# Another distance, within 512 bytes, between the rows of the split operands and the rows of the weights

## The chip, the cores and the metric

One core of a Trainium2 chip. The metric is the device time in microseconds of one execution on that core. The kernel before has a median of 1011.47 us over 3 runs (1011.46, 1011.47 and 1014.0).

## What is computed

Two transformer blocks one after the other, on 256 tokens of width 1024, in float32. The first has two kinds of attention, a merge and a feed-forward part; the second a chunked delta rule, a sparse attention, an output projection `w_out`, a cross-attention to 256 memory tokens and a feed-forward part. What matters here are the dense products in them:

```python
# first block
merged = g_swa * (o_swa @ w_branch_swa[l]) + g_diff * (o_diff @ w_branch_diff[l])
h = h + rms_norm(merged @ w_out[l], post_mix_gain[l])
u = rms_norm(h, pre_ffn_gain[l])
gate_up = u @ w_ffn_in[l]
f = (jax.nn.silu(gate_up[..., :D_FF]) * gate_up[..., D_FF:]) @ w_ffn_out[l]
# second block
x = x + jnp.concatenate([o_dn, o_dsa], axis=-1) @ w_out[l]
hx = rmsnorm(x, g_xattn[l]);  mn = rmsnorm(mem, g_mem[l])
qx = hx @ w_xq[l];  kvx = mn @ w_xkv[l]
x = x + ox @ w_xo[l]
hf = rmsnorm(x, g_ffn[l])
x = x + (jax.nn.silu(hf @ w_gate[l]) * (hf @ w_up[l])) @ w_down[l]
```

## The kernel before

Activations lie transposed, as 8 row tiles of 128 features by 256 tokens (`KT` = 8, `NT` = 256; `NK` = 272 where the 16 meta tokens of the first block stand behind them). A product of an activation with 128 columns of a weight matrix is one call of `gemm` (L316). `load_w` (L301) has SP fetch the 512 KB of those columns into `raw`, ACT round them to float32r (`wh`) and DVE, or POOL in the first stages, subtract to get the rest (`wl`); there are three buffers of each, or more where the planner of the tiles finds room. The activation was split in the same way before, by `split` (L284), into a high part and a low part. `gemm` then issues 24 matmuls into one PSUM tile: for each of the 8 row tiles `wh` against the high part and `wh` against the low part, then for each row tile `wl` against the high part. In each of these matmuls TensorE loads a square of 128x128 weights (stationary) and streams the 256 columns of one row tile of the activation past it (moving). The next square is loaded while a matmul streams.

The split operands, and who uses them:

- `uh`, `ul` from `new_u` (L406): 8 row tiles of `NK` = 272 floats each, so that row tile k begins 1088 k bytes into the tile, and 256 of the 272 are used after the first stage. Made in `post_norm` (L851) for the 44 gemms of the first feed-forward part (`ffn_in`, L871, called at L914), and in `residual` (L1522) for the 8 gemms of `w_xq` (L1565) and for the 44 gemms of the second feed-forward part (L1621). A first pair (L421) feeds the projections of the first block.
- `mem_h`, `mem_l` (L771): 8 row tiles of 256 floats, 1024 bytes each. They are the moving operand in the 8 gemms of `mem_keys` (L787) and the stationary one in `mem_values` (L791, 8 weight tiles with 24 matmuls each at L802 to L804; three of the four groups run at L930, the last is woven into the second block).
- `mix_h`, `mix_l` (L957) for the 8 gemms of `w_out` of the second block (L1536); `ox_h`, `ox_l` (L1553) for the 8 gemms of `w_xo` (L1602).
- `f_h`, `f_l`: moving in `post_norm` for `w_fo1` (L925), stationary in `down` (L1628) for `w_dn`.
- `od_h`/`m_h` and their low parts, and `os_h`, `os_l`, as the moving operand of other gemms.

Where a tile begins is chosen by the planner when the program is built. In the program of the kernel before, counted modulo 512 bytes within a partition, all `raw`, `wh` and `wl` begin at 192, and as a square of weights has rows of 512 bytes, so does every square. Against that the row tiles of the split operands lie, in bytes:

| operand | distance from the weights' rows, modulo 512 |
|---|---|
| `f_h`, `f_l`, `m_h`, `m_l`, `od_h`, `od_l` | -64, the same for every row tile |
| `mem_h`, `mem_l`, `ox_h`, `ox_l` | 0, the same for every row tile |
| `mix_h` / `mix_l` | -64 / 0 |
| `uh`, `ul` of both feed-forward parts | 0, 64, 128, ... 448: 64 more with each row tile (the row tiles are 1088 bytes apart) |
| `uh`, `ul` of `w_xq` | -64, 0, 64, ...: 64 more with each row tile |

Of the kernel before, what the change touches and what calls it, by code (L numbers as in the profile page):

```python
# [17 lines left out]
F32R = mybir.dt.float32r  # L18
# [7 lines left out]
P = 128  # L26
NT = 256
NM = 16
NK = NT + NM
NP = NT + 32  # L30
D = 1024
KT = D // P
FF = 2816
FT = FF // P
# [177 lines left out]
BDLAST = 0  # L212
WARM = 12
RB = 2
MAGIC = float(0x5F3759DF)
# [5 lines left out]
def _program(tc, d, out):  # L221
# [10 lines left out]
    with ctx:  # L232
# [4 lines left out]
        gpool = new_pool(ctx, "gen")  # L237
# [3 lines left out]
        hT = rpool.tile([P, KT, NK], F32, name="hT", tag="resA")  # L241
# [164 lines left out]
        def new_u():  # L406
            uh = gpool.tile([P, KT, NK], F32R, name="uh", tag="uh")
            ul = gpool.tile([P, KT, NK], F32R, name="ul", tag="ul")
            return uh, ul


# [9 lines left out]
        uh, ul = new_u()  # L421
# [6 lines left out]
        for k in range(1, KT, 2):  # L428
            n = min(2, KT - k)
# [16 lines left out]
        rs = gpool.tile([P, NK], F32, name="rs", tag="rs", bufs=2)  # L446
        rsqrt_chain(st[:, :NK], NK, rs)
        us = [(uh[:, k, :NT], ul[:, k, :NT]) for k in range(KT)]
# [34 lines left out]
        at = ExitStack()  # L483
# [286 lines left out]
        mhp = new_pool(mhst, "memhl", side="right")  # L770
        mem_h = mhp.tile([P, 8, NT], F32R, name="mem_h")  # L771
        mem_l = mhp.tile([P, 8, NT], F32R, name="mem_l")
        memt = mhp.tile([P, KT, NT], F32, name="memt")
# [36 lines left out]
        mpool = new_pool(mg, "m")  # L810
# [25 lines left out]

        def post_norm(src_w, xs, gain, res, res_out, g_next, whole=False):

# [9 lines left out]
            if whole:  # L848
                u = gpool.tile([P, KT, NK], F32, name="u", tag="uh")
            else:  # L850
                uh, ul = new_u()  # L851
            acc2 = gpool.tile([P, NK], F32, name="acc2", tag="acc2", bufs=1)[:, :NT]
# [10 lines left out]
            if whole:  # L863
                return [u[:, k, :NT] for k in range(8)], rs2[:, :NT]
            return [(uh[:, k, :NT], ul[:, k, :NT]) for k in range(8)], rs2[:, :NT]

        h1 = rpool.tile([P, KT, NT], F32, name="h1", tag="resB")
        us, rs = post_norm(d["w_out1"], [(m_h[:, k, :], m_l[:, k, :]) for k in range(8)],
                           "post_mix", hT, h1, "pre_ffn")

# [23 lines left out]
        bpool = new_pool(b2, "b")  # L894
# [16 lines left out]
        mpool = new_pool(fst, "f")  # L911
        f_h = mpool.tile([P, FT, NT], F32R, name="f_h")
# [43 lines left out]
        dve.memset(ones_q, 1.0 / 256)  # L956
        mix_h = bpool.tile([P, 8, NT], F32R, name="mix_h")  # L957
        mix_l = bpool.tile([P, 8, NT], F32R, name="mix_l")

# [560 lines left out]

        def residual(src_w, xs, res, res_out, g_next, late=(), more=0):
            uh, ul = new_u()  # L1522
            acc = gpool.tile([P, NK], F32, name="acc", tag="acc", bufs=1)[:, :NT]
# [10 lines left out]

        x2 = rpool.tile([P, KT, NT], F32, name="x2", tag="resB")
        us, rs = residual(d["w_out2"], [(mix_h[:, k, :], mix_l[:, k, :]) for k in range(8)], x1, x2, "g_xattn", (0,1,2,3), 2)  # L1536
        b2.close()

# [13 lines left out]
        values = [two("vx_", vx[:, :, h * NT:(h + 1) * NT]) for h in range(4)]  # L1552
        ox_h = xpool.tile([P, 8, NT], F32R, name="ox_h")  # L1553
        ox_l = xpool.tile([P, 8, NT], F32R, name="ox_l")
        rx = xpool.tile([P, 4], F32, name="rx")
# [45 lines left out]
        x3 = rpool.tile([P, KT, NK], F32, name="x3", tag="resA")[:, :, :NT]  # L1601
        us, rs = residual(d["w_xo"], [(ox_h[:, k, :], ox_l[:, k, :]) for k in range(8)], x2, x3, "g_ffn", (4,5,6,7), 2)  # L1602
        xa.close()
# [9 lines left out]
        for qb in range(2):  # L1613
            for kk_ in range(2):
# [3 lines left out]
                dve.tensor_copy(x3t[:, qb, kk_ * 512:(kk_ + 1) * 512], t)  # L1618
        f_h = mpool.tile([P, FT, NT], F32R, name="f_h")
        f_l = mpool.tile([P, FT, NT], F32R, name="f_l")  # L1620
        ffn_in(mpool, d["w_gu2"], us, rs, f_h, f_l)  # L1621
# [77 lines left out]
```

## Time and profile before

| | |
|---|---|
| median of 3 runs | 1011.47 us (1011.46 to 1014.0) |
| the profiled execution's own time | 1014.09 us |
| its span, first to last instruction | 1012.3 us |
| TensorE matmul busy | 974.1 us, 96% of the span |
| weight loads on TensorE busy | 916.1 us, 90% |
| VectorE, ScalarE, GpSimd busy | 722.8, 544.8, 312.3 us |
| mean granted TensorE clock | 0.984 |

The span lies 1.8 us under the profiled execution's own time. A matmul's record lasts longer than the time to the next one's start, as they are pipelined: a 128x256 record lasts some 280 ns and the next one starts after some 115 ns. What counts for the time is the distance from start to start, which the text calls the pitch.

### The profile page before, as it was taken

Reading aid. Unit: us, or ns where it says so; the run is one execution under the profiler, and the core shown is the slowest. Engines: PE = TensorE matmul, PEld = TensorE weight load, DVE = VectorE, ACT = ScalarE, POOL = GpSimd, SP = SyncE. Lnnn points to the kernel's source line nnn. Section 1 sums busy time; section 2 is a strip of 40 time slices with the busy share of each in tenths; the row PEclk is TensorE's granted clock in tenths of the full one; section 3 lists DMA queues with packets and bytes.
Section 4 is the critical chain, followed back from the end, with each engine's and each line's share of the span. In section 5 each row is a group of like instructions: output and inputs, shape, how many; then the busy total and the mean of one; then the engine's idle time right before and its main releaser. Section 6 shows DMA issues by size and latency. Waiting matters only on the chain. (4 is left out here: it accounts for less than half of the span.)

```text
span 1012.3 us, 18979 instructions
## 1 busy us (share of the span) xinstructions
PE 974.1 (96%) x7356; PEld 916.1 (90%) x7356; DVE 722.8 (71%) x1468; ACT 544.8 (54%) x1089; POOL 312.3 (31%) x294
## 2 busy tenths in 40 slices
PE   9889999999978999999999899999999999999996
PEld 8779999998978999999999788787799999999885
DVE  7998899887697696656455638977687676666444
ACT  4556677666544555555454444335666555555433
POOL 6865468655491032221100302221021002222002
PEclk9998999999997999999999899999999999999998
DMA  6333333333434555555666232333045255555552
GB/s 238 129 104 101 109 107 124 120 110 105 167 125 148 188 204 186 187 187 183 214 200 198 83 133 91 122 114 106 1 150 205 64 186 188 187 187 186 182 192 88
DMA packets 42026, 149.31 MB, mean 147 GB/s; under 512 B 4728, under 2 KB 5376, under 8 KB 41808
## 3 DMA queue, kind: packets, MB, share of 16 engines
q1 hardware_dynamic: 40896, 145.47, 42.6%
q0 software_dynamic: 608, 2.03, 0.7%
q8 instruction: 58, 0.95, 0.4%
q10 hardware_dynamic: 432, 0.59, 0.2%
q14 instruction: 32, 0.26, 0.1%
HBM read 147.01 MB, written 1.06 MB: 146 GB/s over the span
## 5 line engine op out<-in xcount | busy, mean ns | idle before, releaser
L311 ACT ACTIVATE wh<-raw 128x1024 fp32r<-128x1024 f32 (+1 forms) x244 | 256.2, 1052 | 222.7 <-PE mm L326 134.3
L313 DVE TENSOR_TENSOR wl<-raw,wh 128x1024 fp32r<-128x1024 f32 (+1 forms) x220 | 274.0, 1247 | 85.8 <-ACT wh L311 83.7
L326 PE MATMUL mm<-uh,wh 128*128 128x256 f32 (+1 forms) x1112 | 280.5, 287 | 1.3 <-DVE vbm L540 0.9
L326 PE MATMUL mm<-ul,wh 128*128 128x256 f32 (+1 forms) x1112 | 279.0, 286 | 0.2 <-DVE ul L291 0.2
L326 PEld LDWEIGHTS mm<-uh,wh 128*128 128x128 f32 x1112 | 211.1, 190 | 4.6 <-DVE vbm L540 1.1
L326 PEld LDWEIGHTS mm<-ul,wh 128*128 128x128 f32 x1112 | 211.5, 190 | 1.3 <-DVE ul L291 0.5
L326 PE MATMUL mm<-uh,wl 128*128 128x256 f32 (+1 forms) x1112 | 162.5, 285 | 0.0
L326 PEld LDWEIGHTS mm<-uh,wl 128*128 128x128 f32 x1112 | 145.2, 191 | 0.8 <-issue 0.3
L878 POOL TENSOR_TENSOR sg<-sg,rs 128x256 f32<-128x256 f32 x44 | 49.4, 1126 | 233.8 <-ACT sg L877 229.3
L313 POOL TENSOR_TENSOR wl<-raw,wh 128x1024 fp32r<-128x1024 f32 x30 | 72.4, 2414 | 51.9 <-ACT wh L311 51.9
L337 PE MATMUL mm<-u,raw 128*128 128x256 f32 x320 | 73.1, 382 | 0.2 <-DMA raw<-w_pr 0.2
L337 PEld LDWEIGHTS mm<-u,raw 128*128 128x128 f32 x320 | 59.5, 190 | 9.5 <-DVE y L995 0.6
L882 DVE TENSOR_TENSOR ft<-mm,sg 128x256 f32<-128x256 f32 x42 | 17.8, 424 | 52.0 <-PE mm L326 51.5
L326 PE MATMUL mm<-f_h,wh 128*128 128x256 f32 x176 | 41.1, 276 | 0.0
L326 PE MATMUL mm<-f_l,wh 128*128 128x256 f32 x176 | 41.1, 276 | 0.0
L876 DVE TENSOR_TENSOR sg<-mm,rs 128x256 f32<-128x256 f32 x40 | 17.0, 424 | 31.4 <-PE mm L326 31.3
L1633 PE MATMUL ac<-wh,f_h 128*128 128x512 f32 (+1 forms) x110 | 38.4, 349 | 0.0
L1636 PE MATMUL ac<-wh,f_l 128*128 128x512 f32 (+1 forms) x110 | 38.1, 347 | 0.0
L1637 PE MATMUL ac<-wl,f_h 128*128 128x512 f32 (+1 forms) x110 | 37.8, 347 | 0.0
L326 PEld LDWEIGHTS mm<-f_l,wh 128*128 128x128 f32 x176 | 33.0, 188 | 0.0
L326 PEld LDWEIGHTS mm<-f_h,wh 128*128 128x128 f32 x176 | 33.0, 188 | 0.0
L855 POOL TENSOR_TENSOR x<-fg,h 128x256 f32<-128x256 f32 x8 | 7.7, 997 | 66.6 <-PE mm L804 66.6
(544 smaller groups left out, 2205.8 us busy)
## 6 DMA issues: line engine op xcount, KB each, us to landing
raw<-w_gu SPq DMA_DIRECT2D x88, 512.0 KB, 4.3
raw<-w_dn SPq DMA_DIRECT2D x22, 512.0 KB, 3.7
raw<-w_pr SPq DMA_DIRECT2D x20, 512.0 KB, 3.6
raw<-w_gate SPq DMA_DIRECT2D x16, 512.0 KB, 3.6
raw<-w_out SPq DMA_DIRECT2D x16, 512.0 KB, 3.7
raw<-w_fo SPq DMA_DIRECT2D x16, 512.0 KB, 3.8
raw<-w_kb SPq DMA_DIRECT2D x8, 512.0 KB, 3.7
raw<-w_vb SPq DMA_DIRECT2D x8, 512.0 KB, 3.7
```

The costliest lines, as they stand in the source:

```text
L311: act.activation(h[:, :kt * c], raw[:, :kt * c], AF.Copy)
L313: eng.tensor_tensor(l[:, :kt * c], raw[:, :kt * c], h[:, :kt * c].bitcast(F32), OP.subtract)
L326: pe.matmul(o, w[:, k * P:(k + 1) * P], xs[k][i], start=(first and n_ == 0), stop=(last and n_ == len(steps) - 1))
L337: pe.matmul(o, raw[:, k * P:(k + 1) * P], x, start=(k == 0), stop=(k == len(xs) - 1))
L855: pool.tensor_tensor(res_out[:, j, :], fg[:, j, :], res[:, j, :NT], OP.add)
L876: dve.tensor_tensor(sg, o, rs, OP.mult)
L878: pool.tensor_tensor(sg, sg, rs, OP.mult)
L882: dve.tensor_tensor(t, o, sg, OP.mult)
L1633: m = pe.matmul(o, f_h[:, k, tok], h[:, cols], start=(k == 0), stop=False)
L1636: pe.matmul(o, f_l[:, k, tok], h[:, cols], start=False, stop=False)
L1637: pe.matmul(o, f_h[:, k, tok], l[:, cols], start=False, stop=(k == FT - 1))
```

## The change

The 8 row tiles of an operand are laid out 1024 bytes apart, from a given number of floats (`AT`) after the tile's begin. For `uh` and `ul` the tile keeps its size of 8 x 272 floats and the row tiles no longer have the 16 unused floats between them; `mem`, `mix`, `ox` and `f` get 128 floats more per partition. No instruction is added or removed by the text of the kernel. The first pair of `uh`, `ul` (L421) and the unsplit `u` of the second block (L849) stay as they are.

```diff
+AT = {'ffn1': 32, 'xatt': 48, 'ffn2': 64, 'mem_h': 96, 'mem_l': 96, 'mix_h': 64, 'mix_l': 64, 'ox_h': 96, 'ox_l': 96, 'f': 0}
...
+        def rows_at(t, at):
+
+            return t[:, at:at + KT * NT].rearrange("p (a b) -> p a b", a=KT)
+
+        def new_u_at(at):
+            return [rows_at(gpool.tile([P, KT * NK], F32R, name="u" + e, tag="u" + e), at) for e in "hl"]
+
+        def parts_at(pool_, name, at_h, at_l):
+            return [rows_at(pool_.tile([P, KT * NT + P], F32R, name=name + e), at)
+                    for e, at in (("_h", at_h), ("_l", at_l))]
...
-        mem_h = mhp.tile([P, 8, NT], F32R, name="mem_h")
-        mem_l = mhp.tile([P, 8, NT], F32R, name="mem_l")
+        mem_h, mem_l = parts_at(mhp, "mem", AT["mem_h"], AT["mem_l"])
...
-        def post_norm(src_w, xs, gain, res, res_out, g_next, whole=False):
+        def post_norm(src_w, xs, gain, res, res_out, g_next, at=0, whole=False):
...
-                uh, ul = new_u()
+                uh, ul = new_u_at(at)
...
-                           "post_mix", hT, h1, "pre_ffn")
+                           "post_mix", hT, h1, "pre_ffn", at=AT["ffn1"])
...
-        mix_h = bpool.tile([P, 8, NT], F32R, name="mix_h")
-        mix_l = bpool.tile([P, 8, NT], F32R, name="mix_l")
+        mix_h, mix_l = parts_at(bpool, "mix", AT["mix_h"], AT["mix_l"])
...
-        def residual(src_w, xs, res, res_out, g_next, late=(), more=0):
-            uh, ul = new_u()
+        def residual(src_w, xs, res, res_out, g_next, late=(), more=0, at=0):
+            uh, ul = new_u_at(at)
...
-        ox_h = xpool.tile([P, 8, NT], F32R, name="ox_h")
-        ox_l = xpool.tile([P, 8, NT], F32R, name="ox_l")
+        ox_h, ox_l = parts_at(xpool, "ox", AT["ox_h"], AT["ox_l"])
...
-        f_h = mpool.tile([P, FT, NT], F32R, name="f_h")
-        f_l = mpool.tile([P, FT, NT], F32R, name="f_l")
+        f_h, f_l = (mpool.tile([P, FT * NT + P], F32R, name=n)[:, AT["f"]:AT["f"] + FT * NT].rearrange(
+            "p (a b) -> p a b", a=FT) for n in ("f_h", "f_l"))
```

The two calls of `residual` (L1536 and L1602) get `AT["xatt"]` and `AT["ffn2"]`. The last hunk is the `f_h`, `f_l` of the second block (L1619); those of the first stay. In bytes the table's numbers are 128 (`ffn1`), 192 (`xatt`), 256 (`ffn2`, `mix`) and 384, which is -128 modulo 512 (`mem`, `ox`). The distances that the change is described by are +128, +256, -128, +192 and -192 bytes.

## Rows read from the trace of the kernel before

**Rows 1.** The page: span, busy time by engine, TensorE's clock in 40 slices.

```profile
span 1012.3 us, 18979 instructions
PE 974.1 (96%) x7356; PEld 916.1 (90%) x7356; DVE 722.8 (71%) x1468; ACT 544.8 (54%) x1089; POOL 312.3 (31%) x294
PEclk9998999999997999999999899999999999999998
```

**Rows 2.** Windows of both feed-forward parts and `w_fo1`: length, busy (instructions) by engine, clock.

```profile
core 0: us, PE busy (x) PEld busy (x) DVE busy (x) ACT busy (x) POOL busy (x), PEclk, DMA share, GB/s
400.00:480.00 80.00, 80.00 (x679) 80.00 (x678) 48.56 (x71) 41.92 (x57) 16.25 (x14) 1.00 0.54 186
500.00:548.00 48.00, 48.00 (x426) 48.00 (x425) 24.09 (x26) 22.98 (x33) 0.00 (x0) 1.00 0.68 216
...
835.00:935.00 100.00, 100.00 (x847) 100.00 (x846) 62.60 (x91) 52.61 (x72) 21.39 (x18) 1.00 0.54 185
```

**Rows 3.** The chain that ended last: the second feed-forward part's matmuls.

```profile
827.13 116.44 PE mm L326 x984
```

**Rows 4.** Waits: who waited for whom, us in total, times, longest.

```profile
ACT wh L311 <- PE mm L326: 134.3, 123, 4.5
DVE wl L313 <- ACT wh L311: 83.7, 66, 4.9
...
ACT wh L311 <- DMA raw<-w_gu: 9.7, 4, 3.7
```

**Rows 5.** Timeline, PE: runs of `wl` matmuls at -64 (start us, us).

```profile
323.30 1.07 PE L326 MATMUL mm<-m_h,wl 128*128 128x256 f32 x8
...
513.32 1.07 PE L326 MATMUL mm<-f_h,wl 128*128 128x256 f32 x8
```

**Rows 6.** Timeline, PE: runs of `wl` matmuls at 0.

```profile
361.60 1.12 PE L326 MATMUL mm<-mem_h,wl 128*128 128x256 f32 x8
...
806.80 1.12 PE L326 MATMUL mm<-ox_h,wl 128*128 128x256 f32 x8
...
809.68 1.13 PE L326 MATMUL mm<-ox_h,wl 128*128 128x256 f32 x8
```

**Rows 7.** Timeline, PE: the same runs in the first feed-forward part.

```profile
384.96 1.11 PE L326 MATMUL mm<-uh,wl 128*128 128x256 f32 x8
387.80 1.11 PE L326 MATMUL mm<-uh,wl 128*128 128x256 f32 x8
390.64 1.11 PE L326 MATMUL mm<-uh,wl 128*128 128x256 f32 x8
```

**Rows 8.** Timeline, PE: one step of `w_dn`, its 256-column matmuls.

```profile
951.02 0.28 PE L1633 MATMUL ac<-wh,f_h 128*128 128x256 f32 x1
951.14 0.28 PE L1636 MATMUL ac<-wh,f_l 128*128 128x256 f32 x1
...
951.73 0.40 PE L1633 MATMUL ac<-wh,f_h 128*128 128x512 f32 x1
```

**Rows 9.** Windows of the `mix`, `mem_values` and cross-attention stages.

```profile
741.00:757.00 16.00, 16.00 (x139) 16.00 (x139) 14.98 (x23) 11.25 (x21) 6.02 (x4) 1.00 0.53 178
...
556.00:600.00 44.00, 39.59 (x232) 36.62 (x231) 22.74 (x54) 16.43 (x40) 7.71 (x8) 0.92 0.33 111
...
758.00:800.00 42.00, 40.85 (x336) 39.98 (x336) 27.80 (x66) 22.73 (x47) 5.43 (x4) 1.00 0.44 151
800.00:827.00 27.00, 27.00 (x229) 26.95 (x228) 22.57 (x38) 17.75 (x29) 0.00 (x0) 1.00 0.36 120
```

**Rows 10.** Groups by shape, PE: busy us, mean ns, idle before and releaser.

```profile
L802 PE MATMUL mm<-wh,mem_h 128*128 128x256 f32 x64 | 19.4, 303 | 0.7 <-ACT wh L311 0.7
L804 PE MATMUL mm<-wl,mem_h 128*128 128x256 f32 x64 | 19.4, 303 | 5.0 <-DVE wl L313 5.0
...
L326 PE MATMUL mm<-f_h,wh 128*128 128x256 f32 x176 | 41.1, 276 | 0.0
...
L326 PE MATMUL mm<-od_h,wh 128*128 128x256 f32 x64 | 15.3, 280 | 0.0
L326 PE MATMUL mm<-m_h,wh 128*128 128x256 f32 x64 | 15.0, 281 | 0.0
```

More of the change, by code (lines that the diff above doesn't have):

```diff
@@ L1535, in _program @@
         x2 = rpool.tile([P, KT, NT], F32, name="x2", tag="resB")
-        us, rs = residual(d["w_out2"], [(mix_h[:, k, :], mix_l[:, k, :]) for k in range(8)], x1, x2, "g_xattn", (0,1,2,3), 2)
+        us, rs = residual(d["w_out2"], [(mix_h[:, k, :], mix_l[:, k, :]) for k in range(8)], x1, x2, "g_xattn", (0,1,2,3), 2, AT["xatt"])
         b2.close()
@@ L1601, in _program @@
         x3 = rpool.tile([P, KT, NK], F32, name="x3", tag="resA")[:, :, :NT]
-        us, rs = residual(d["w_xo"], [(ox_h[:, k, :], ox_l[:, k, :]) for k in range(8)], x2, x3, "g_ffn", (4,5,6,7), 2)
+        us, rs = residual(d["w_xo"], [(ox_h[:, k, :], ox_l[:, k, :]) for k in range(8)], x2, x3, "g_ffn", (4,5,6,7), 2, AT["ffn2"])
         xa.close()
```

## The prediction

> **What bounds the kernel now.** I read the page first: TensorE's matmuls cover 96% of the span and no other engine more than 71%, with the clock at its upper level, 2.4 GHz, nearly everywhere [rows 1]. Then the windows by stage: in the two feed-forward parts and in `w_fo1` TensorE is busy for 80.00 of 80, 100.00 of 100 and 48.00 of 48 us, at a granted clock of 1.00 [rows 2], and the chain of waits runs through 984 matmuls there without a break [rows 3]. The waits say the same from the other side: ACT's casts wait for a matmul to give a `wh` buffer back 123 times, 134.3 us in all, and for a weight DMA only four times, 9.7 us [rows 4]. So the time is the number of matmuls times their pitch from start to start, and a change that leaves the number alone can only act on the pitch.
>
> The pitch is what the reader should take from the windows. A matmul that merely reaches into a window is counted, so the pitch is (window + one record of 0.28 us) / count. `w_fo1`: 48.28/426 = 113.3 ns. First feed-forward part: 80.28/679 = 118.2 ns; second: 100.28/847 = 118.4 [rows 2], and 116.44/984 = 118.3 by the chain [rows 3]. The instructions are the same: 128x128 weights, 256 columns, the same type, the same clock, TensorE never idle. What differs is where the streamed rows lie. In the timeline eight `wl` matmuls with operands at -64 take 1.07 us, (1.07 - 0.28)/7 = 113 ns [rows 5]; at 0 they take 1.12, 120 ns, and a whole gemm of 24 takes 809.68 - 806.80 = 2.88 us, 120.0 ns [rows 6]. With `uh`, whose distance goes through all eight multiples of 64, a gemm takes 2.84 us, 118.3 ns [rows 7]. `w_dn` streams the weights and holds the activation, at +64 between the two: its six 256-column matmuls take 951.73 - 951.02 = 0.71 us, 118 ns [rows 8]. `mix`, alternately at -64 and 0, has 16.28/139 = 117.1 [rows 9], about the mean of the two. So the trace has two distances held throughout, -64 at 113.3 ns and 0 at 120.0, and none of those that the change uses.
>
> **The change part by part.** Nothing is added to any queue by the kernel's text: no instruction, wait or DMA. Three things change.
>
> First, the row tiles of `uh`, `ul` lie 1024 instead of 1088 bytes apart, so that the distance is one value through the whole gemm: 44 + 44 gemms of 24 matmuls in the feed-forward parts, 2112, and 192 in `w_xq`. By the table and the placement of before it is +128 (first part), +256 (second) and +192 or +128 (`w_xq`).
>
> Second, `mem` goes from 0 to -128 (192 matmuls in `mem_keys`, and 192 in `mem_values`, where it is the stationary side, so +128 there), `ox` from 0 to -128 (192), and `mix` from -64/0 to +192/+256 (192). With those, 3072 matmuls are moved, of 7356 on TensorE [rows 1]. `f` has offset 0: no change, and `w_fo1` and `w_dn` stay.
>
> Third, the `mem`, `mix`, `ox` and second `f` tiles are 512 bytes longer per partition, which could cost a spare buffer elsewhere. I take nothing: 512 moves no neighbour's distance, and in the feed-forward parts the buffers are handed back by TensorE, the bound. If the cover goes, the cost is like the largest wait of a matmul group on a weight split, 5.0 us before L804 [rows 10]; I put 0 to 2 us of that into the range, since only small stages are tight for room.
>
> The **price of the unseen distances**. Their bounds are the two held distances: 113.3 ns below, 120.0 above. I take 114. What is slow is the coincidence, at 0; the distances of the change are 128 to 256 bytes off on either side, so farther from 0 than the row at -64, which I therefore take as the nearest in kind. I add 0.7 ns, since operands at -64 that run beside other work have somewhat longer records, `od` 280 and `m` 281 ns against 276 for `f` [rows 10]. Against it: +64 in `w_dn` is no nearer to 0 than -64 and has 118, with the roles exchanged [rows 8].
>
> Sum: feed-forward parts 2112 x (118.3 - 114.0) = 9.1 us; `w_xq` 192 x 4.3 = 0.8; `mem_keys` 192 x 6.0 = 1.2; `mem_values` another 1.2, of which I count 0.6, because TensorE idles there for the weight splits, busy 39.59 of 44 us [rows 9, 10]; `mix` 192 x (117.1 - 114.0) = 0.6; `ox` 192 x 6.0 = 1.2. Together 13.5. All of it lies on TensorE's path: the windows of `mix` and `w_xo` are full, 16.00 of 16 and 27.00 of 27 us [rows 9]. What a quicker TensorE asks of the rest is covered: the feed-forward parts need 118.3/114.0 = 1.04 times their 186 GB/s, 193, and `w_fo1` has 216 with TensorE full; ACT's 41.92 and DVE's 48.56 of 80 us become 54% and 63% [rows 2].
>
> The profiled execution's own time is 1014.09 us, 2.6 over the median of the runs shown, 1011.47. From its own time the sum gives 1000.6; against the median, which I forecast, 1011.5 - 13.5 = 998.0 us. At 113.3 for all: 10.6 + 1.0 + 1.3 + 0.6 + 0.7 + 1.3 = 15.5, or 996.0.
>
> The rows show, then, that a matmul beside a weight load is 6.7 ns dearer at one placement than at another [rows 5, 6]. The Trainium skill, TensorE: Matmul & The Clock Gate, section "Step-by-step: what each phase is for", speaks against any such thing: TensorE has two independent SBUF read ports, and "Loading the next tile's weights doesn't steal SBUF read bandwidth from the running matmul." By that rule this change is worth nothing, 1011.5 us; the trace does not agree with it.
>
> **The rivals.**
>
> *Only half of it.* One of the two feed-forward distances is good and the other as now: 13.5 - 4.5 = 9.0 us less, 1002.5. For it: +64 and -64 differ.
>
> *The mean stays.* If each distance has its own price and they add up, the eight in `uh` average 118.3; without -64 and 0 the other six average (8 x 118.3 - 113.3 - 120.0)/6 = 118.9. `mix` near the mean of its two speaks for this. Then `uh` loses 2304 x 0.6 = 1.4, `mix` 192 x 1.8 = 0.3, and `mem` and `ox` gain 576 x 1.1 = 0.6: 1012.6 us.
>
> *It does nothing.* The 118.3 comes from something other than the distance, such as the casts beside it, and stays: 1011.5 us. Against it: the casts run just as much during `w_fo1` at 113.3 [rows 2]. The like of it is that the planner puts the tiles elsewhere: the table alone gives no -192, so some tile must begin at another place than before.
>
> *Slower: the feed-forward distances are as bad as 0.* +128 and +256 held through a gemm repeat one collision 24 times, where now it changes with each row tile. At 120.0: 2112 x 1.7 = 3.6, `w_xq` 0.3, `mix` 192 x 2.9 = 0.6, `mem` and `ox` nothing: 1011.5 + 4.5 = 1016.0 us. It decides from a pitch of 118.3 + 3.0/2112 us = 119.7 ns. For it: the one other held distance of the trace, 0, is at 120.0, above the mixture.
>
> **How the numbers follow.** The forecast has 0.50 and half of it 0.12; the mean stays 0.13, nothing 0.10; slower 0.15. A difference under 0.3%, 3.0 us, could not be told from no change. Faster is then 0.62, same 0.23, slower 0.15. The range begins at 993: 996.0 for all at 113.3, and 1 ns on 3000 matmuls below that, as -64 need not be the best distance. It ends at 1014: the cases at 1011.5 and 1012.6 with up to 2 us for a lost buffer are in, most of the slower one is out. The forecast's own range is 993 to 1001.
>
> **What would show it.** In the changed kernel's windows, 80 us of a feed-forward part should hold 80.28/0.114 = 704 matmuls instead of 679, a gemm should take 2.74 us instead of 2.84, eight `wl` matmuls 1.08, `w_fo1` still 2.72 per 24. `mem` and `ox` runs of 1.12 us should shrink to 1.08. TensorE should stay busy throughout; were it to wait there for a cast or a DMA, the cover was misjudged. I am wrong if the two feed-forward parts stay at 118 or go to 120 ns, or differ by several ns from each other.

## The result, and the profile after

The changed kernel has a median of 1017.66 us over 5 runs (1016.42 to 1020.44), the kernel before beside it 1012.69 us over 5 (1011.46 to 1014.0). The ratio is 1.0057, with a 95% interval of 1.0045 to 1.0069: 0.57% slower, outside the predicted range of 993 to 1014. The profiled execution is the longest of the five, 1020.44 us with a span of 1018.7; that of before was at 1014.09, so that these two traces differ by 6.4 us where the medians differ by 5.0. Four executions of the runs below took 1342 to 5343 us (one each of ffn1_back, ffn2_only, mirror and the kernel before) and are left out of the ratios.

In the program as built, `ox` lies at -192 and both parts of `mix` at +192, where the prediction had -128 and +192/+256: the planner began these tiles elsewhere. The other operands that the prediction moves lie where it says, `w_xq`'s `uh` at +128.

The page of the changed kernel, against [rows 1]:

```profile
span 1018.7 us, 18978 instructions
PE 979.5 (96%) x7356; PEld 921.6 (90%) x7356; DVE 724.1 (71%) x1468; ACT 544.3 (53%) x1089; POOL 311.4 (31%) x294
PEclk9999999999998999999999899999999999999999
```

The same matmuls and weight loads are on TensorE, both 5.4 or 5.5 us dearer, at a mean granted clock of 0.983 (0.984 before). Its windows, with the columns of [rows 2]; the third is for `mix` and stands against the first of [rows 9]. Under them the chain of waits, against [rows 3]:

```profile
400.00:480.00 80.00, 80.00 (x677) 80.00 (x676) 48.52 (x72) 41.41 (x56) 16.19 (x14) 1.00 0.57 185
500.00:548.00 48.00, 48.00 (x410) 48.00 (x409) 22.32 (x24) 22.71 (x31) 0.00 (x0) 1.00 0.66 206
746.00:762.00 16.00, 16.00 (x138) 16.00 (x137) 15.19 (x24) 11.28 (x20) 6.24 (x4) 1.00 0.53 184
835.00:935.00 100.00, 100.00 (x835) 100.00 (x835) 62.22 (x93) 53.83 (x74) 21.68 (x19) 1.00 0.54 188
```

```profile
832.57 118.08 PE mm L328 x984
```

TensorE is still full everywhere that it was full. The pitch, (window + 0.28) / count, is 80.28/677 = 118.6 ns in the first feed-forward part (118.2 before), 48.28/410 = 117.8 in `w_fo1` (113.3 before, and nothing of its own was moved), 16.28/138 = 118.0 in `mix` (117.1), and 118.08/984 = 120.0 in the second part by the chain (118.3). The waits say that nothing else has become the bound; they answer to [rows 4]:

```profile
ACT wh L313 <- PE mm L328: 139.6, 124, 4.5
...
ACT wh L313 <- DMA raw<-w_gu: 10.6, 6, 3.8
```

And the timeline of TensorE, runs of `wl` matmuls of `m` (in `w_out1`), of `mem`, of the first part, of `w_fo1`, `ox` and the second part, then 256-column matmuls of `w_dn`; they answer to [rows 5 to 8]:

```profile
324.18 1.10 PE L328 MATMUL mm<-m_h,wl 128*128 128x256 f32 x8
...
359.64 1.11 PE L328 MATMUL mm<-mem_h,wl 128*128 128x256 f32 x8
362.48 1.11 PE L328 MATMUL mm<-mem_h,wl 128*128 128x256 f32 x8
...
385.99 1.11 PE L328 MATMUL mm<-uh,wl 128*128 128x256 f32 x8
388.84 1.11 PE L328 MATMUL mm<-uh,wl 128*128 128x256 f32 x8
...
504.82 1.10 PE L328 MATMUL mm<-f_h,wl 128*128 128x256 f32 x8
...
812.31 1.10 PE L328 MATMUL mm<-ox_h,wl 128*128 128x256 f32 x8
815.13 1.10 PE L328 MATMUL mm<-ox_h,wl 128*128 128x256 f32 x8
...
840.09 1.12 PE L328 MATMUL mm<-uh,wl 128*128 128x256 f32 x8
842.97 1.12 PE L328 MATMUL mm<-uh,wl 128*128 128x256 f32 x8
...
952.55 0.28 PE L1643 MATMUL ac<-wh,f_h 128*128 128x256 f32 x1
...
952.89 0.28 PE L1643 MATMUL ac<-wh,f_h 128*128 128x256 f32 x1
```

From the start of one `wl` run to that of the next there are 24 matmuls: `mem` 2.84 us, 118.3 ns by these two rows and 118.6 over all (120.0 before), first part 2.85/24 = 118.8, `ox` 2.82/24 = 117.5 (120.0 before), second part 2.88/24 = 120.0. The `wl` run of `w_fo1` lasts 1.10 us, 117 ns from start to start by (1.10 - 0.28)/7, where [rows 5] have 1.07; so does that of `m`, also at -64 and also with 1.07 in [rows 5]. In `w_dn` three matmuls of 256 columns take 952.89 - 952.55 = 0.34 us, 113 ns, where they took 118 before; its distance is +64 in both kernels.

The stages' prices in this trace: second part 1056 x 1.7 ns = +1.8 us, `w_fo1` 528 x 4.5 = +2.4, first part 1056 x 0.4 = +0.4, `mix` +0.2; `w_dn`, 131 matmuls of 256 columns, -0.6, `ox` -0.4, `mem_keys` -0.25. Together +3.5 of the 6.4 us. Of the rest 0.8 us have arisen by 256 us, in stages that the change doesn't touch, and 1.9 between `w_fo1` and `mix`; the second profile, below, does not show the 1.9 again.

### The profile page after: what moved, and what is told of

Its sections match the earlier page's. It is cut to its first block, busy times and chain, and to the rows that moved or that the text cites. A ratio compares the mean times of both kernels' runs of the same rounds, so it can differ in the third digit from the quotient of the medians.

```text
span 1018.7 us, 18978 instructions
## 1 busy us (share of the span) xinstructions
PE 979.5 (96%) x7356; PEld 921.6 (90%) x7356; DVE 724.1 (71%) x1468; ACT 544.3 (53%) x1089; POOL 311.4 (31%) x294
## 4 chain that ended last, share of the span: by engine, by line
PE 76%; DVE 14%; POOL 3%; ACT 3%; issue 2%; DMA 2%; SPq 0%; ACTq 0%; DVEq 0%; POOLq 0%
PE mm L328 48%; PE mm L339 5%; PE s L328 3%; PE s L530 2%; DVE wl L315 2%; PE ac L1647 2%; PE ac L1646 2%; PE ac L1643 2%; POOL memt L793 1%; DVE fg L866 1%; PE o L610 1%; POOL memt L795 1%; DVE ul L293 1%; ACT wh L313 1%; PE mm L1406 1%
## 5 line engine op out<-in xcount | busy, mean ns | idle before, releaser
L313 ACT ACTIVATE wh<-raw 128x1024 fp32r<-128x1024 f32 (+1 forms) x244 | 256.3, 1052 | 225.1 <-PE mm L328 139.6
```

The source lines that it names most:

```text
L313: act.activation(h[:, :kt * c], raw[:, :kt * c], AF.Copy)
```

## The experiments

The theories, as the expectations name them. **A**: each distance has one price of its own, unknown ahead of the run. **B**: a distance held through a stage has several steady pitches, and how the stage is entered settles which. **Rival C** in the first four expectations: to hold any distance is what costs, a changing one is better; in the later ones: a stage's pitch is settled by chance in each run. In the trace a held pitch is a short pattern of start-to-start intervals, in ns, that repeats: 113, 113, 114 at 113.3; 117 to 119 at 117.8; at +128 mostly the five intervals 115, 117, 122, 120, 119, with a mean of 118.6; 120 each time at 0 and 256, with one other pattern of the same mean at 0 in the second part of the sweep.

**The changed kernel again, unaltered** (rep_after).

> The changed kernel once more, unaltered, to see what repeats. Theory A (each distance has one price, whatever went before): all pitches as in its first profile: first feed-forward part 118.6 ns, w_fo1 117.8 although its distance of -64 was not touched, second feed-forward part 120.0; then w_fo1's 113.3 before the change needs another cause. Theory B (one distance has several steady pitches, and the state in which a stage is entered picks one): the two feed-forward parts repeat, but w_fo1, at -64, may come out at 113.3 or at 117.8, 2.4 us apart over its 528 matmuls.

One run, 1017.34 us. Windows of `w_fo1` and of the second part:

```profile
500.00:540.00 40.00, 40.00 (x342) 40.00 (x342) 18.65 (x20) 18.94 (x26) 0.00 (x0) 1.00 0.69 208
...
835.00:920.00 85.00, 85.00 (x710) 85.00 (x710) 52.82 (x78) 44.80 (x62) 19.02 (x17) 1.00 0.57 185
```

40.28/342 = 117.8 and 85.28/710 = 120.1 ns, as in the first profile. But `mix`, at the same +192, ran at 113.3 instead of 117.8: one program, one distance, two pitches.

**Everything at -64** (all64), the price on which the prediction rested:

```diff
-AT = {'ffn1': 32, 'xatt': 48, 'ffn2': 64, 'mem_h': 96, 'mem_l': 96, 'mix_h': 64, 'mix_l': 64, 'ox_h': 96, 'ox_l': 96, 'f': 0}
+AT = {'ffn1': 112, 'xatt': 0, 'ffn2': 112, 'mem_h': 112, 'mem_l': 112, 'mix_h': 0, 'mix_l': 0, 'ox_h': 0, 'ox_l': 0, 'f': 0}
```

> Every split operand that the change moves is put at -64 bytes instead, the distance at which the kernel before ran 113.3 ns. Theory A, with 113.3 as the price of -64: both feed-forward parts go from 118.6 and 120.0 to 113.3 ns (2112 matmuls), w_xq, mem, mix and ox too: some 17 to 20 us less than the changed kernel, about 998, faster than both. Theory B: -64 can also settle at 117.8 ns, and a stage that is entered so stays so: between 1000 and 1014, with stages at one of the two values and nothing in between. Rival C (the unchanging distance itself costs, against rows that move on by 64): no better than 1012.

1011.62 us, ratio to before 0.9989 (0.9979 to 0.9999). The chain of the second part:

```profile
825.17 115.89 PE mm L328 x984
```

115.89/984 = 117.8 ns. `w_fo1` and nearly all of the first part are at 117.8 too, `mem_keys` at 113.3 until a stall before its last gemms. (A stall is here a place where a matmul starts 200 ns or more behind the one before it.) So -64 is not a distance at 113.3 ns: it is one with two pitches, and the trace of before had shown one of them.

**The first feed-forward part as before** (ffn1_back).

```diff
-                uh, ul = new_u_at(at)
+                uh, ul = new_u()
```

> The changed kernel with one part undone: the first feed-forward part again with rows 1088 bytes apart, so eight distances in turn. Theory A: that part goes from 118.6 to 118.3 ns, 1056 x 0.3 = 0.3 us less, and w_fo1 behind it stays as it was. Theory B: the same 0.3 us, and w_fo1, entered from another state, can go back from 117.8 to 113.3 ns, 2.4 us less: in all 2.7 us below the changed kernel.

1014.9 us, ratio 1.0016 (1.0004 to 1.0028). The window of `w_fo1`:

```profile
500.00:540.00 40.00, 40.00 (x355) 40.00 (x354) 19.42 (x21) 19.67 (x29) 0.00 (x0) 1.00 0.68 215
```

40.28/355 = 113.5 ns: `w_fo1`, whose own operands lie as in the changed kernel, is quick again. So its own operands don't settle its pitch; that the part before it does is argued from this one profile, and after5, below, shows that it is not the whole. With that part undone 2.8 of the 5.0 us go, by the sums 0.4 for its own pitch and 2.4 for that of `w_fo1`.

**All distances in one run** (sweep): `uh` at 0, and the weights moved from gemm to gemm.

```diff
+D1 = [-64, -64, -64, -64, -64, -64, -64, -64, -64, 0, 0, 0, 0, 0, 64, 64, 64, 64, 64, 128, 128, 128, 128, 128, 192, 192, 192, 192, 192, 256, 256, 256, 256, 256, -192, -192, -192, -192, -192, -128, -128, -128, -128, -128]
...
-            h = wpool.tile([P, KT * P], F32R, name="wh", tag="wh" + tag, bufs=3)
+            h = wpool.tile([P, KT * P + P], F32R, name="wh", tag="wh" + tag, bufs=3)[:, woff:woff + KT * P]
...
-                gemm(src_w[2 * j], us, NT, use_g, ps=bank(0))
+                gemm(src_w[2 * j], us, NT, use_g, ps=bank(0), woff=off(2 * j))
```

> In both feed-forward parts the activation's rows are held at one place, and the weight tiles of each gemm are moved instead, so that one run shows the pitch at many distances. First part, by 64 bytes: 9 gemms at -64, then 5 each at 0, 64, 128, 192, 256, -192 and -128. Second part, by 16 bytes: 4 gemms each at -128, -112, ... -16, 0, 16, 32. Theory A: each distance at the price seen for it: -64 113.3 ns, 0 120.0, 128 118.6, 192 117.8, 256 120.0, -192 117.8, -128 118.6 (within 0.2), and 64 somewhere from 113 to 119. Theory B: the distances from 128 on as said, -64 at 113.3 or 117.8. Finer steps: if the cost is that of crossing a line of memory, the pitch changes in steps between -128 and 32, lowest near -64; if it is a phase that locks, it runs smoothly or jumps between the same few values.

One run, 1009.92 us. Timeline of the first part, two neighbouring `wl` runs at -64, 0, +64, +128, +192, 256, -192 and -128 in turn:

```profile
388.83 1.07 PE L330 MATMUL mm<-uh,wl 128*128 128x256 f32 x8
391.55 1.07 PE L330 MATMUL mm<-uh,wl 128*128 128x256 f32 x8
...
400.14 1.12 PE L330 MATMUL mm<-uh,wl 128*128 128x256 f32 x8
403.02 1.12 PE L330 MATMUL mm<-uh,wl 128*128 128x256 f32 x8
...
411.39 1.07 PE L330 MATMUL mm<-uh,wl 128*128 128x256 f32 x8
414.11 1.07 PE L330 MATMUL mm<-uh,wl 128*128 128x256 f32 x8
...
425.20 1.11 PE L330 MATMUL mm<-uh,wl 128*128 128x256 f32 x8
428.05 1.12 PE L330 MATMUL mm<-uh,wl 128*128 128x256 f32 x8
...
442.23 1.11 PE L330 MATMUL mm<-uh,wl 128*128 128x256 f32 x8
445.06 1.11 PE L330 MATMUL mm<-uh,wl 128*128 128x256 f32 x8
...
453.63 1.12 PE L330 MATMUL mm<-uh,wl 128*128 128x256 f32 x8
456.51 1.12 PE L330 MATMUL mm<-uh,wl 128*128 128x256 f32 x8
...
467.76 1.07 PE L330 MATMUL mm<-uh,wl 128*128 128x256 f32 x8
470.48 1.07 PE L330 MATMUL mm<-uh,wl 128*128 128x256 f32 x8
...
481.57 1.11 PE L330 MATMUL mm<-uh,wl 128*128 128x256 f32 x8
484.42 1.12 PE L330 MATMUL mm<-uh,wl 128*128 128x256 f32 x8
```

Start to start, by 24: 113.3, 120.0, 113.3, 118.8, 117.9, 120.0, 113.3, 118.8 ns. The reader should see the symmetry: 0 and 256 are the worst, +128 and -128 alike, and the odd multiples of 64 are at 113.3 or 117.8. At -64 the first gemms of this run were at 117.8, until a stall; then 113.3. The second part went through -128 to +32 in steps of 16 bytes: 116.7 to 120.0 ns, nothing at 113.3.

**Put into the quick pitch** (kick, and its twin nokick). Both parts at +64 and -192, everything else at -64; weights placed by `woff` floats as in the sweep. In kick the parts' first two gemms lie at 0 and at 256, 64 bytes below. The twin has `FIRST = 0`.

```diff
+AT = {'ffn1': 16, 'xatt': 0, 'ffn2': 80, 'mem_h': 112, 'mem_l': 112, 'mix_h': 0, 'mix_l': 0, 'ox_h': 0, 'ox_l': 0, 'f': 0}
+FIRST = 16
...
+                gemm(src_w[2 * j], us, NT, use_g, ps=bank(0), woff=FIRST * (j == 0))
+                gemm(src_w[2 * j + 1], us, NT, use_u, ps=bank(1), woff=FIRST * (j == 0))
```

> Both feed-forward parts held at distances that showed 113.3 ns in the sweep, +64 (first part) and -192 (second); only their first two gemms have their weights 64 bytes further on, so that they run at 0 and at 256. Everything else at -64, as in all64 (1011.6 us). Theory B (a held odd multiple of 64 has two steady pitches, 113.3 and 117.8 ns, and what runs right before settles which): after 0 and after 256 the sweep came out at 113.3, so both parts should run at 113.3: 1011.6 - 2112 x 4.5 ns = 1002 us, and if w_fo1 then comes out at 113.3 too, 528 x 4.5 ns less, near 1000. Theory A (one price for each distance): +64 and -192 are at 113.3 whatever precedes them, so this one and its twin without the two gemms have the same time, near 1002. Rival C (a stage's pitch is settled by chance in each run, and what precedes it doesn't matter): the pitches come out mixed and the times of one kernel spread over 5 us or more.

> The twin of the kernel before it: the first two gemms of each feed-forward part at the part's own distance, +64 and -192, and nothing else changed. Theory B: nothing puts these parts into the quick state; entered from a stall or from mem_keys they land at either pitch, most likely 117.8 as in all64, then about 1011 us; the difference to the twin is 2112 x 4.5 = 9.5 us if both parts land slow, half of that if one does. Theory A: the same time as its twin, near 1002 us. Rival C: a spread of several us from run to run and the same median as the twin.

kick 1001.38 us, ratio 0.9886 (0.987 to 0.9901); nokick 1006.63 us (1004.57 to 1012.39), ratio 0.9947 (0.9926 to 0.9968). The chains of the second part, kick first:

```profile
820.80 111.52 PE mm L329 x984
```

```profile
822.50 115.89 PE mm L329 x984
```

111.52/984 = 113.3 ns against 117.8, by where the weights of two gemms lie; every tile of the two programs begins at the same place, and neither has a stall in the second part behind those gemms. That part differs by 4.4 us between the profiles, the medians by 5.2. Theory A falls.

The first part is no such test, since stalls settle its pitch. These are `wl` runs of kick behind its gemm at 0, behind a stall at 376 us, and behind one at 382 us (there TensorE does two other matmuls, and starts some 411 and 222 ns apart follow):

```profile
374.67 1.07 PE L329 MATMUL s<-uh,wl 128*128 128x256 f32 x8
...
377.88 1.10 PE L329 MATMUL mm<-uh,wl 128*128 128x256 f32 x8
...
384.39 1.07 PE L329 MATMUL mm<-uh,wl 128*128 128x256 f32 x8
```

So its two gemms did lead to 113.3, but the first stall undid that and the second brought it back, and the twin went over from 117.8 to 113.3 at the same second stall. In all eight profiles with this part at one odd multiple of 64 there, the pitch changes over at that stall: to 113.3 in kick, nokick, kick2, kick3, kick4 and the sweep, to 117.8 in all64 and in mirror, which follows.

**Both steps turned round** (mirror): the first two gemms again at 0 and 256, the parts 64 bytes below instead of above.

```diff
-AT = {'ffn1': 16, 'xatt': 0, 'ffn2': 80, 'mem_h': 112, 'mem_l': 112, 'mix_h': 0, 'mix_l': 0, 'ox_h': 0, 'ox_l': 0, 'f': 0}
-FIRST = 16
+AT = {'ffn1': 112, 'xatt': 0, 'ffn2': 48, 'mem_h': 112, 'mem_l': 112, 'mix_h': 0, 'mix_l': 0, 'ox_h': 0, 'ox_l': 0, 'f': 0}
+FIRST = 112
```

> The kernel kick with both steps turned round: the first two gemms of each feed-forward part again at 0 and 256, but the part itself 64 bytes below instead of above, at -64 (first part) and +192 (second). Theory B with the rule of the step of +64: a step of -64 leads to the slow pitch (w_fo1 went from 0 to -64 and stayed at 117.8), so the second part runs at 117.8, the first too unless a stall among its first gemms turns it over (as one did for the kernel without the two gemms): about 1001.4 + 4.7 = 1006.1 us, or 1011 if both stay slow. If any stretch at 0 or 256 makes the quick state, 113.3 and 1001.4 us. Theory A: -64 at 113.3 as in the first feed-forward part's neighbours of the kernel before, +192 at the 117.8 of the sweep: the first part quick, the second slow, 1006 us as well; it differs from B in the first part alone, and in w_fo1.

1010.68 us, ratio 0.9977 (0.9964 to 0.9991). The window of the first part and the chain of the second:

```profile
400.00:480.00 80.00, 80.00 (x682) 80.00 (x681) 48.92 (x71) 41.44 (x56) 16.93 (x15) 1.00 0.58 187
```

```profile
825.12 115.89 PE mm L329 x984
```

80.28/682 = 117.7 and 117.8 ns: both slow. In the first part this is again the work of stalls, as its `wl` runs behind the gemm at 0, behind the first stall and behind the second show:

```profile
374.04 1.10 PE L329 MATMUL s<-uh,wl 128*128 128x256 f32 x8
...
377.27 1.07 PE L329 MATMUL mm<-uh,wl 128*128 128x256 f32 x8
...
383.72 1.10 PE L329 MATMUL mm<-uh,wl 128*128 128x256 f32 x8
```

Right behind the step, before any stall, both parts were slow where kick's were quick. It is not that a stretch at 0 or 256 helps, but that the step from it goes up by 64. (The sweep had one step up by 64 that did not help: from +128 to +192, 117.9.)

**`w_fo1` in the changed kernel** (f_kick, f_kick2): the first chunk of its weights, 24 matmuls, elsewhere, so that `f` begins at 0 (112 floats) or at -128 (16 floats) and then goes to its -64.

```diff
-                gemm_long(src_w[j], xs, NT, use)
+                gemm_long(src_w[j], xs, NT, use, 112 if len(xs) > 8 and j == 0 else 0)
```

> The changed kernel, with the weights of the first chunk of 16 matmuls and its 8 low ones of w_fo1 448 bytes further on, so that f runs them at 0 and then goes back to -64, where it was. Theory B: the 117.8 ns of w_fo1 in the changed kernel is not the price of -64 but what +128 in the part before it left behind; with 24 matmuls at 0 in between it goes back to 113.3, 504 x 4.5 ns = 2.3 us less than the changed kernel's 1017.7, 1015.4 us. If 0 does not lead to the quick pitch for -64 (only +64 after 0 was seen), it stays at 117.8 and 1017.7. Theory A has no reason for any change but 24 x 2 ns.

> The changed kernel with the first chunk of w_fo1 at -128 instead of 0 (f_kick had 0, and w_fo1 stayed at 117.8). Theory B with the rule of the step of +64: w_fo1 goes back to the 113.3 ns that it had before the change, 504 x 4.5 = 2.3 us less than f_kick or the changed kernel: 1012.4 to 1015.4 us. Theory A: 117.8 as in f_kick, no gain.

f_kick 1014.69 us, ratio 1.0018 (1.0008 to 1.0027); f_kick2 1012.02 us, ratio 0.9992 (0.9981 to 1.0003). Windows of `w_fo1`, f_kick first:

```profile
500.00:540.00 40.00, 40.00 (x342) 40.00 (x342) 19.06 (x20) 18.31 (x26) 0.00 (x0) 1.00 0.67 214
```

```profile
500.00:540.00 40.00, 40.00 (x355) 40.00 (x355) 19.39 (x22) 19.13 (x27) 0.00 (x0) 1.00 0.69 212
```

117.8 and 113.5 ns; the medians differ by 2.7 us where 2.3 was expected. But f_kick, with the slow pitch, was already 3 us under the changed kernel, which theory B doesn't explain (after_wide, below, does).

**Parts of the change alone**: the second feed-forward part (ffn2_only, against the kernel before), and everything but the feed-forward parts (small_only, against the changed kernel).

```diff
-            uh, ul = new_u()
+            uh, ul = new_u() if at is None else new_u_at(at)
...
-        us, rs = residual(d["w_xo"], [(ox_h[:, k, :], ox_l[:, k, :]) for k in range(8)], x2, x3, "g_ffn", (4,5,6,7), 2)
+        us, rs = residual(d["w_xo"], [(ox_h[:, k, :], ox_l[:, k, :]) for k in range(8)], x2, x3, "g_ffn", (4,5,6,7), 2, 64)
```

```diff
-                uh, ul = new_u_at(at)
+                uh, ul = new_u()
...
-            uh, ul = new_u_at(at)
+            uh, ul = new_u() if at == AT["ffn2"] else new_u_at(at)
```

> The kernel before with one part of the change: the uh, ul of the second feed-forward part at +256, the rest as before. Theory A and B: that part goes from 118.3 to 120.0 ns, 1056 x 1.7 = 1.8 us more; w_dn behind it, at an unchanged +64, is entered from a held distance and goes from 118 to 113 or 114 ns on its 256-column matmuls, about 0.7 us less: 1013.0 + 1.1 = 1014.1 us. w_fo1 stays at 113.3. By the step of the prediction that failed (a distance away from 0 costs 114 ns) it would be 1013.0 - 1056 x 4.3 ns = 1008.5 us.

> The changed kernel with both feed-forward parts as before (row tiles 1088 bytes apart), so that mem, mix, ox and the uh of w_xq alone are moved. By their pitches (mem_keys 118.7 instead of 120.0, ox 117.8 instead of 120.0, mix 113.3 or 117.8 instead of 116.7, w_xq 118.8 as before): 0.3 to 1 us less, 1012.0 us, and w_fo1 at 113.3. By subtraction (the change's +5.0, less 2.8 that went with the first feed-forward part and 1.3 for the second): 0.9 us more, 1013.5 us. By the prediction's step (all at 114): 1.2 + 0.6 + 0.6 + 1.2 + 0.8 = 4.4 less, 1008.2 us.

ffn2_only 1013.91 us, ratio 1.0009 (1.0 to 1.0017); small_only 1012.74 us, ratio 1.0003 (0.9994 to 1.0013). By the medians the first is 1.3 us over the kernel before; for the second no difference can be told. ffn2_only's second part in the chain:

```profile
825.06 118.08 PE mm L326 x984
```

120.0 ns, and `w_dn` behind it at 113 to 114, as in the changed kernel. `w_fo1` is at 113.3 in both.

**More places** (kick2, kick3). kick2 is kick with the first chunk of `w_fo1` and one gemm of `w_out2` at -128 and the last gemm of the second part at 256. Of kick2 the three places, and of kick3, which is kick with the distance of each part kept on through the stage behind it:

```diff
+                gemm_long(src_w[j], xs, NT, use, 16 if len(xs) > 8 and j == 0 else 0)
...
+                gemm(src_w[2 * j + 1], us, NT, use_u, ps=bank(1), woff=FIRST * (j in ends))
...
+                gemm(src_w[j], xs, NT, use, ps=ps, late=late if j < 2 + more else (), woff=FIRST * (j == kick))
```

```diff
-                gemm_long(src_w[j], xs, NT, use)
+                gemm_long(src_w[j], xs, NT, use, 96 if len(xs) > 8 else 0)
...
-            w = load_w(d["w_dn"][k], KT, tag="" if k < FT - LAST else "_last")
+            w = load_w(d["w_dn"][k], KT, tag="" if k < FT - LAST else "_last", woff=64)
```

> The kernel kick (1001.4 us) with three more places put into the quick state, each by running the gemm before it, or its first chunk, at a distance 64 bytes lower: the first chunk of w_fo1 at -128 (then -64), the gemm of w_out2 before the four last ones at -128 (then -64), the last gemm of the second feed-forward part at 256 (before w_dn at +64). Theory B, with the rule so far read from the runs that a step of +64 from 0, 256 or -128 leads to the quick pitch (0 to +64, 256 to -192, -128 to -64 did): w_fo1 113.3 instead of 117.8, 504 x 4.5 = 2.3 us; the last four gemms of w_out2 113.3, 0.4 us; the 131 matmuls of 256 columns of w_dn 113 to 114 instead of 118, 0.5 us: 998.2 us. If -128 doesn't lead to the quick pitch for f (it did in the sweep, at the end of the first part), 1001 us. Rival C: no difference beyond the spread, 1001.4.

> The kernel kick (1001.4 us; w_fo1 and w_dn at 117.8 there, since they change the distance once more), with the weights of w_fo1 384 bytes and those of w_dn 256 bytes further on, so that w_fo1 runs at the +64 of the part before it and w_dn at the -192 of the part before it. Theory B: where the distance doesn't change and TensorE has no stall, the quick pitch carries over, as the slow one did in all64 from the first feed-forward part to w_fo1: 528 x 4.5 = 2.4 us less in w_fo1, and 131 x 4.3 = 0.6 us in w_dn: 998.4 us. If a new stage settles its pitch anew (another PSUM tile, another operand), 117.8 can come again: 1001. Theory A: f at +64 and w_dn at -192 at 113.3, the same number as B; it has already failed on kick and its twin.

kick2 1000.48 us (ratio 0.9885), kick3 1000.98 us (ratio 0.9887). `w_fo1`, kick2 first:

```profile
500.00:540.00 40.00, 40.00 (x342) 40.00 (x341) 20.66 (x22) 19.42 (x27) 0.00 (x0) 1.00 0.64 190
```

```profile
500.00:540.00 40.00, 40.00 (x342) 40.00 (x342) 20.36 (x22) 19.72 (x27) 0.00 (x0) 1.00 0.63 189
```

117.8 both times, and `w_dn` at 118 both times; the last gemms of `w_out2` in kick2 stayed at 117.8 too. Both expectations failed: one chunk at -128 does not do behind a part at 113.3 what it did behind one at 118.7, and at an unchanged +64 the quick pitch is lost where `f` takes the place of `uh`. So "a step up by 64" is no general rule, and the distance modulo 512 is not all that counts.

**The changed kernel beside one with longer weight tiles** (after5, unaltered; after_wide, with `wh` and `wl` 512 bytes longer as in f_kick, and all distances kept).

```diff
-            h = wpool.tile([P, KT * P], F32R, name="wh", tag="wh" + tag, bufs=3)
-            l = wpool.tile([P, KT * P], F32R, name="wl", tag="wl" + tag, bufs=3)
+            h = wpool.tile([P, KT * P + P], F32R, name="wh", tag="wh" + tag, bufs=3)[:, woff:woff + KT * P]
+            l = wpool.tile([P, KT * P + P], F32R, name="wl", tag="wl" + tag, bufs=3)[:, woff:woff + KT * P]
```

> The changed kernel with the wh and wl tiles 512 bytes longer and nothing else: every distance as in the changed kernel, no stretch at another one. It is the base that f_kick and f_kick2 were made from. If the longer tiles alone, by where the planner then puts the small ones, give the 3.0 us by which f_kick (w_fo1 still at 117.8) lay under the changed kernel: 1014.7 us. If they do nothing: 1017.5 us, and f_kick had its gain from elsewhere, such as w_out2 at 113.3 in its profile.

> The changed kernel once more, unaltered, beside the two others on one chip. Theory B: w_fo1 at 117.8 and the second feed-forward part at 120.0 again, 1016.4 to 1018 us. The account so far, from single parts: second feed-forward part +1.3 us, mem, mix, ox and w_xq +0.2, first part with w_fo1 +2.8 (0.4 for the part's own 118.7 ns, 2.4 for w_fo1): +4.3 over the kernel before, 1016.9 us.

after5 1017.58 us (1015.0 to 1019.45, 9 runs), ratio 1.0043 (1.0028 to 1.0058); after_wide 1014.47 us, ratio 1.0013 (1.0 to 1.0025). The longer tiles give f_kick's 3 us, and f_kick2, with `w_fo1` quick, lies 2.4 us under after_wide. They move many small tiles; which of them counts was not tried. The window of `w_fo1` in after5:

```profile
500.00:540.00 40.00, 40.00 (x355) 40.00 (x354) 19.82 (x21) 19.49 (x29) 0.00 (x0) 1.00 0.68 215
```

113.5 ns, in the unaltered changed kernel, and `mix` at 113.3 as well. This profiled execution is the shortest of the nine, 1015.0 us; the one with `w_fo1` at 117.8 and `mix` at 113.3 had 1017.34, the one with both at 117.8 had 1020.44. Behind a part at +128 `w_fo1` can land at either pitch, and this is where the spread of the changed kernel comes from, in part.

**`w_fo1` behind changing distances** (kick4). In all four profiles where the first part ended with the distance changing by 64 from row tile to row tile, `w_fo1` was quick. kick4 is kick with the weights of the last two gemms of that part 576 instead of 512 bytes apart, and the last two of the second part at 256.

```diff
+            if spread:
+                h, l = (t.rearrange("p (a b) -> p a b", a=KT)[:, :, :P] for t in (h, l))
...
+                gemm(src_w[2 * j], us, NT, use_g, ps=bank(0), woff=FIRST * (j == 0 or j == last), spread=(j == FT - 1 != last))
```

> The kernel kick (1001.4 us), with the weights of the last two gemms of the first feed-forward part laid 576 instead of 512 bytes apart, so that the distance goes through all eight multiples of 64 there, as it did through the whole part in the kernel before, and with the last two gemms of the second part at 256. In all four profiles in which w_fo1 followed on such a part (before, ffn1_back, ffn2_only, small_only) it ran at 113.3; in kick, kick2 and kick3, behind a part at 113.3, it ran at 117.8. If the last gemms before a stage settle it: w_fo1 at 113.3, 2.4 us less, and w_dn at 113 to 114 behind 256 as in every profile of the change, 0.5 us less: 998.5 us. If two gemms are too few and what counts is the state the long stretch was in (as one gemm at 256 did nothing for w_dn in kick2): both at 117.8 and 1001.4 us.

998.43 us (997.72 to 1002.02, 4 runs), ratio 0.9856 (0.9838 to 0.9875), the fastest kernel here. The profiled execution is the longest of the four, 1002.02 us, so that the one profile does not show the faster three. Its window of `w_fo1` and its chain of the second part:

```profile
500.00:540.00 40.00, 40.00 (x356) 40.00 (x355) 20.75 (x22) 19.98 (x27) 0.00 (x0) 1.00 0.66 202
```

```profile
819.86 111.84 PE mm L336 x984
```

40.28/356 = 113.1 ns in `w_fo1`. `w_dn` stayed at 118: two gemms at 256 before it were too few, while behind 44 it was at 113 to 114 in every profile.

The pitches of the long stages in all profiles, in ns, each from its window, chain or starts (before an arrow: until a stall):

| kernel | first part | `w_fo1` | second part | `w_dn`, 256 columns |
|---|---|---|---|---|
| before, small_only | changing: 118.3 | 113.3 | changing: 118.3 | 118 |
| ffn1_back, ffn2_only | changing: 118.3 | 113.3 | +256: 120.0 | 113 |
| changed, rep_after, after_wide, f_kick | +128: 118.7 | 117.8 | +256: 120.0 | 113 |
| after5; f_kick2 (behind -128) | +128: 118.7, 120.0 in a few gemms | 113.3 | +256: 120.0 | 113 |
| sweep | in turn, -128 last: 118.8 | 113.3 | in turn, +32 last: 116.7 | 118 |
| all64 | -64: 117.8 -> 113.3 -> 117.8 | 117.8 | -64: 117.8 | 114 |
| mirror | -64: 117.8 -> 113.3 -> 117.8 | 117.8 | +192: 117.8 | 118 |
| nokick | +64: 117.8 -> 113.3 | 117.8 | -192: 117.8 | 118 |
| kick, kick2, kick3 | +64: 113.3 -> 117.8 -> 113.3 | 117.8 | -192: 113.3 | 118 |
| kick4 | +64: 113.3 -> 117.8 -> 113.3 | 113.3 | -192: 113.3 | 118 |

(Both stalls of the first part lie within its first four gemms. `w_fo1` is at -64 and `w_dn` at +64 throughout, but at +64 and -192 in kick3.) What follows: B in part. A distance held at an odd multiple of 64 bytes has two pitches, 113.3 and 117.8; at 0 and 256 it has 120.0; at +128 118.7, but 120.0 in two gemms of after5 and f_kick2. The two gemms ahead settled the second part in kick against its twin, and most likely `w_fo1` in kick4, seen in one profile. A stall can turn the pitch over. No rule covers all rows, and after5 shows that some entries are left to chance, as the later rival C has it.

## Why the prediction was wrong

**What held.** TensorE is the bound, its pitch is what the placement acts on, and the formula for the pitch reads it. What the pitch gains comes out in the time: kick, with both parts at 113.3, lies 11 us under the kernel before. The cover held: ACT's casts still wait for matmuls, 139.6 us in all, and for a `w_gu` DMA 10.6, and in kick4 TensorE is full at 113.3 ns in both feed-forward parts and in `w_fo1`. That a matmul beside a weight load is dearer at one placement than at another held on every run, 113.3 to 120.0 ns at a granted clock of 1.00. The Trainium skill, TensorE: Matmul & The Clock Gate, "Step-by-step: what each phase is for", has two independent read ports, by which a weight load takes no read bandwidth from a running matmul; it has no such price, and the runs do not agree with it.

**The step that failed** is the "price of the unseen distances", "I take 114". Two things in it were wrong. First, "What is slow is the coincidence, at 0": 256 is a coincidence as well, at the same 120.0, and -128 and +128 stand at 118.7 and more; distance from 0 is not what makes a row tile cheap. Second, that a held distance has a price at all which one row can show: -64, the "nearest in kind", has two, and [rows 5] show the one that these stages had landed on. The evidence against it was in the prediction, `w_dn` with 118 at +64 [rows 8], and was set aside as the roles exchanged. In the sum, the 9.1 us to be gained in the two parts came out as losses of 0.4 and 1.8 us; of the gains, `mem_keys` had 0.25 for 1.2, `ox` 0.4 for 1.2, `mix` between 0.2 lost and 0.6 gained for 0.6, and mem, mix, ox and `w_xq` together nothing that small_only could tell, for 4.4.

**A second step**: "`w_fo1` and `w_dn` stay". Their placement did; their pitch did not. `w_fo1` lost 2.4 us in four of the six profiles with the first part at +128 (f_kick and f_kick2 have a stretch of their own between), and `w_dn` gained 0.6 behind +256. A stage that a change doesn't touch was costed at nothing with no look at what runs just ahead of it.

**A smaller one**: "I take nothing: 512 moves no neighbour's distance". As built, the longer tiles had `ox` begin at another place, and the operand `os` ahead of `w_out1` as well; in `w_out1` the first 72 matmuls ran at 117.8 instead of 113.6, 0.3 us, in all six profiles with these tiles and the weight tiles of before, and at 113.6 in the twelve others. That `os` is the cause was not tested.

**The rivals.** "Slower", with a chance of 0.15, gave 1016.0 us and came nearest, with its condition half met: the second part went to 120.0, past its 119.7, the first only to 118.7, and the rest came from `w_fo1`. "The mean stays" had 118.9 for +128, near the 118.7 measured, but not 256. The account by single parts: second part +1.3 us, first part with `w_fo1` +2.8, the others +0.2, together 4.3 of 5.0.

**What stays open.** Which reads meet which in the memory was not tested, and neither was what, beside the distance modulo 512, the gemms ahead and the stalls, settles a pitch (kick3's `w_fo1`). The 3.1 us between after5 and after_wide come from where other tiles lie; the 0.3 us of `w_out1` are in them, and no run names the rest.

## What to carry to other kernels

A full TensorE can have a pitch that depends on where its two streams lie to each other; look for it by dividing windows of equal work by their counts, and test a placement by holding it through a stage in a run, since one row at a good pitch does not make the placement good. When a placement is changed, look at the pitch of the stages behind it as well, and at several profiles of one program. Here the gain of 1.4% came not from the distance alone but from a distance together with what happens ahead of it: a few gemms at another distance in the second part and before `w_fo1`, a stall in the first part.

## What was not expected of the hardware

The same instruction, a float32r matmul of 128x128 by 256 columns at a granted clock of 1.00, has steady pitches of 113.3, 117.8, 118.7 and 120.0 ns, and a stage keeps one of them for 40 us and more. At 2.4 GHz 113.3 ns are 272 cycles and 120.0 are 288, 16 and 32 more than the 256 columns. Two of the pitches belong to one distance, and one program showed both: `w_fo1` at 117.8 and at 113.3, `mix` at 117.8 and at 113.3. And one stall, with starts some 411 and 222 ns apart, turned the pitch over in all eight profiles that meet it at an odd multiple of 64, six times to 113.3 and twice to 117.8.
